# Expert sum of a hybrid decoder layer: 768 output columns of the second 128 tokens summed on VectorE from gathered expert rows

## The chip, the core and the metric

The kernel runs on one core of a Trainium2 chip. The metric is the device time of one execution in microseconds (us). Before the change, three runs took 2298.72, 2300.01 and 2301.34 us (median 2300.01).

## What is computed

One decoder layer for 256 tokens of width 2048, all in float32: a token mixer (sliding-window attention and an mLSTM, gated and merged), then a channel mixer of 16384 single-neuron experts. The change touches only the last part:

```python
# s_top, i_top: top 16 of 128 keys, for 8 heads and 2 halves; the 16 best of their 256 sums
idx   = ...                                # (256 tokens, 8 heads, 16): expert numbers
gates = softmax(top_s)                     # the same shape
u   = peer_u[idx]                          # expert rows, 2048 wide
act = gelu(einsum('td,thkd->thk', x, u))
out = einsum('thk,thkd->td', gates * act, peer_v[idx])
```

So each token has 128 slots (8 heads x 16); each slot is an expert with a weight, gate times gelu of a product, and the output is the weighted sum of the slots' rows of `peer_v`.

## The kernel before

The kernel does not gather expert rows. It multiplies all tokens with all 16384 rows of `peer_u`, multiplies gelu of that with a grid of gates that is zero where a token did not choose the expert, and multiplies the result with all of `peer_v`. Everything is a dense matrix product on TensorE.

A float32 matrix is split into two parts of TensorE's input type: `hi` (a rounded copy, made by ScalarE, L84) and `lo` (the remainder, made by VectorE, L85). A product is then three matmuls: hi by hi, hi by lo, lo by hi. All large matrices stream through the same buffers: `load` (L89) brings 128 rows of 1024 columns (512 KB) into one of four `raw` buffers by a DMA from SP's queue, `parts_of` splits them into two `hi` and two `lo` parts of 512 columns (four buffers each).

The stages follow each other: the mixer to about 690 us, the queries and scores to about 790, the u stage (128 expert blocks, each 128 rows of `peer_u`) to 1594, and the last stage with `peer_v` to the end.

- **u stage** (`ws_units`, L160 to L162): the weights stand, 256 tokens move. Per block 48 matmuls of 256 columns. The result, `z`, times the norm's factor goes to SBUF (L757), ScalarE takes its gelu (L748 or L750), and the product with the gates is kept for all blocks in `wA` and `wB` (128 experts of a block x 256 tokens). Beside it run the choice of the top 16 and `scatter` (L828 to L853), which spreads four tokens' gates over the grid: ScalarE and VectorE build one-hot factors in `ab` buffers, TensorE multiplies them.
- **Last stage** (`v_consume`, L865 to L880): per block the weights `wv(i)` are split into `ph` and `pl`, and stand on TensorE; the 2048 columns of `peer_v` move, 512 at a time. There are two halves of the tokens (t = 0, 1), so a block is 4 x 2 x 3 = 24 matmuls of 512 columns. The sums stay in all eight PSUM banks for the whole stage: `sd` for the first 128 tokens, `mm` for the second. At the end VectorE adds the residual `x1` (L891) and SP stores.

Work that may wait is kept in a list (`side`) and handed out between the units at a rate. Each engine then executes its instructions in one fixed order, which a scheduler computes from the program; an instruction whose wait is not yet fulfilled holds up all behind it on its engine.

## Time and profile before

| | |
|---|---|
| median of three runs | 2300.01 us |
| span of the profiled execution | 2296.5 us |
| TensorE busy | 2265.1 us, 99% |
| VectorE, ScalarE, GpSimd busy | 71%, 58%, 3% |
| DMA | 416.24 MB, 181 GB/s in the mean |
| last stage | 1594 to 2291 us |

The span is that of one execution taken by the profiler; the time of a run holds the start and the end of the program too. A busy TensorE counts a matmul from its start to its modelled end; since matmuls overlap, the time that one costs in a full queue is read from counts in a stretch, not from its duration. DMA-issuing instructions are not counted as busy time of the engine that issues them.

### The profile page before, as it was taken

Reading aid. Unit: us, or ns where it says so; the run is one execution under the profiler, and the core shown is the slowest. Engines: PE = TensorE matmul, PEld = TensorE weight load, DVE = VectorE, ACT = ScalarE, POOL = GpSimd, SP = SyncE. Lnnn points to the kernel's source line nnn. Section 1 sums busy time; section 2 is a strip of 40 time slices with the busy share of each in tenths; the row PEclk is TensorE's granted clock in tenths of the full one; section 3 lists DMA queues with packets and bytes.
Section 4 is the critical chain, followed back from the end, with each engine's and each line's share of the span. In section 5 each row is a group of like instructions: output and inputs, shape, how many; then the busy total and the mean of one; then the engine's idle time right before and its main releaser. Section 6 shows DMA issues by size and latency. Waiting matters only on the chain.

```text
span 2296.5 us, 41687 instructions
## 1 busy us (share of the span) xinstructions
PE 2265.1 (99%) x15441; PEld 2093.2 (91%) x15441; DVE 1640.0 (71%) x3436; ACT 1343.3 (58%) x2915; POOL 64.2 (3%) x79
## 2 busy tenths in 40 slices
PE   7999999999999999999999999999999999999998
PEld 6987799999999999999999999999888888888887
DVE  8977787677779996755677777786655555555555
ACT  6756566566554445554777777775555555555554
POOL 3000000000010020200000000000000000000000
PEclk9999999999999999999999999999999999999999
DMA  6565545556665545555554555556666666665665
GB/s 213 182 196 168 150 156 165 180 181 189 212 219 181 164 157 190 174 183 181 166 164 157 165 161 162 164 159 209 195 193 194 194 193 193 193 195 192 194 193 172
DMA packets 115339, 416.24 MB, mean 181 GB/s; under 512 B 12992, under 2 KB 13120, under 8 KB 114752
## 3 DMA queue, kind: packets, MB, share of 16 engines
q1 hardware_dynamic: 115136, 413.59, 56.5%
q8 instruction: 120, 1.97, 0.3%
q14 instruction: 83, 0.68, 0.1%
HBM read 409.35 MB, written 4.19 MB: 180 GB/s over the span
## 4 chain that ended last, share of the span: by engine, by line
PE 91%; DVE 6%; ACT 1%; issue 1%; POOL 0%; DMA 0%; DVEq 0%; SPq 0%; POOLq 0%; ACTq 0%
PE mm L162 17%; PE mm L160 17%; PE mm L161 17%; PE mm L880 5%; PE mm L878 5%; PE sd L878 5%; PE sd L880 5%; PE sd L879 5%; PE mm L879 5%; PE sd L841 2%; DVE lo L85 2%; PE mm L185 2%; PE mm L186 2%; PE mm L187 2%; ACT hi L84 1%
## 5 line engine op out<-in xcount | busy, mean ns | idle before, releaser
L85 DVE TENSOR_TENSOR lo<-raw,hi 128x512 fp32r<-128x512 f32 x1524 | 1056.2, 695 | 564.4 <-ACT hi L84 537.4
L84 ACT ACTIVATE hi<-raw 128x512 fp32r<-128x512 f32 x1524 | 954.4, 629 | 766.3 <-PE mm L161 374.4
L160 PE MATMUL mm<-xh,hi 128*128 128x256 f32 x3088 | 883.3, 286 | 9.9 <-ACT hi L84 7.4
L162 PE MATMUL mm<-xh,lo 128*128 128x256 f32 x3088 | 877.8, 284 | 9.3 <-DVE lo L85 8.9
L161 PE MATMUL mm<-xl,hi 128*128 128x256 f32 x3088 | 874.8, 283 | 1.1 <-DVE xl L85 1.1
L162 PEld LDWEIGHTS mm<-xh,lo 128*128 128x128 f32 x3088 | 592.2, 192 | 14.3 <-DVE lo L85 13.9
L160 PEld LDWEIGHTS mm<-xh,hi 128*128 128x128 f32 x3088 | 592.8, 192 | 11.5 <-ACT hi L84 8.1
L161 PEld LDWEIGHTS mm<-xl,hi 128*128 128x128 f32 x3088 | 592.9, 192 | 2.1 <-DVE xl L85 1.8
L879 PE MATMUL sd<-lo,ph 128*128 128x512 f32 x512 | 199.2, 389 | 0.0
L878 PE MATMUL sd<-hi,ph 128*128 128x512 f32 x512 | 199.2, 389 | 0.0
L878 PE MATMUL mm<-hi,ph 128*128 128x512 f32 x512 | 199.2, 389 | 0.0
L879 PE MATMUL mm<-lo,ph 128*128 128x512 f32 x512 | 199.2, 389 | 0.0
L880 PE MATMUL sd<-hi,pl 128*128 128x512 f32 x512 | 199.2, 389 | 0.0
L880 PE MATMUL mm<-hi,pl 128*128 128x512 f32 x512 | 199.2, 389 | 0.0
L880 PEld LDWEIGHTS mm<-hi,pl 128*128 128x128 f32 x512 | 96.1, 188 | 20.0
L878 PEld LDWEIGHTS mm<-hi,ph 128*128 128x128 f32 x512 | 96.1, 188 | 20.0
L879 PEld LDWEIGHTS sd<-lo,ph 128*128 128x128 f32 x512 | 96.1, 188 | 20.0
L880 PEld LDWEIGHTS sd<-hi,pl 128*128 128x128 f32 x512 | 96.1, 188 | 19.9
L879 PEld LDWEIGHTS mm<-lo,ph 128*128 128x128 f32 x512 | 96.1, 188 | 19.9
L878 PEld LDWEIGHTS sd<-hi,ph 128*128 128x128 f32 x512 | 96.1, 188 | 19.9
L835 ACT ACTIVATE ab<-iot,i1T 128x128 f32<-128x128 f32 x256 | 89.7, 387 | 0.5 <-DVE i1T L811 0.5
L185 PE MATMUL mm<-hi,xh 128*128 128x512 f32 x224 | 89.4, 400 | 0.0
(272 smaller groups left out, 2436.3 us busy)
## 6 DMA issues: line engine op xcount, KB each, us to landing
raw<-u SPq DMA_DIRECT2D x256, 512.0 KB, 3.8
raw<-v SPq DMA_DIRECT2D x256, 512.0 KB, 4.6
raw<-w_g SPq DMA_DIRECT2D x64, 512.0 KB, 4.0
raw<-w_tok SPq DMA_DIRECT2D x56, 512.0 KB, 4.2
raw<-w_qk SPq DMA_DIRECT2D x32, 512.0 KB, 3.9
raw<-w_o SPq DMA_DIRECT2D x32, 512.0 KB, 4.5
raw<-w_pq SPq DMA_DIRECT2D x32, 512.0 KB, 3.9
raw<-w_pa SPq DMA_DIRECT2D x16, 512.0 KB, 3.6
```

The costliest lines, as they stand in the source:

```text
L84: S.activation(hi, src, AF.Copy)
L85: V.tensor_sub(lo, src, hi.bitcast(F32))
L160: PE.matmul(ps, hi[:, w], xh[:, k], start=(k == 0), stop=False)
L161: PE.matmul(ps, hi[:, w], xl[:, k], start=False, stop=False)
L162: PE.matmul(ps, lo[:, w], xh[:, k], start=False, stop=(k == kts - 1))
L185: PE.matmul(ps, xh[:, k, ts], hi, start=(k == 0), stop=False)
L186: PE.matmul(ps, xh[:, k, ts], lo, start=False, stop=False)
L187: PE.matmul(ps, xl[:, k, ts], hi, start=False, stop=(k == KT - 1))
L835: S.activation(B, iot, AF.Square, bias=i1T[:, t:t + 1])
L878: PE.matmul(o, ph[:, ts], hi, start=(i == 0), stop=False)
L879: PE.matmul(o, ph[:, ts], lo, start=False, stop=False)
L880: PE.matmul(o, pl[:, ts], hi, start=False, stop=(i == NE - 1))
```

## The change

In the last stage the second 128 tokens keep 1280 of their 2048 columns on TensorE: in each block, for the third group of 512 columns only 256 move for them, for the fourth none. The other 768 columns come from gathered rows. In the u stage, each block's `z` of the second 128 tokens is stored to DRAM (`zd`) from ScalarE's queue, before gelu, which now writes to a buffer of its own (`gz`); the `zu` buffers go from two to four, the `ab` buffers from eight to six. When the choice of experts is done, `addresses` writes each slot's expert number and its address in `zd` to DRAM.

After the u stage these are read back into the space of `x2h` and `x2l` (named `xh` and `xl` in rows). GpSimd then issues indirect DMAs, 128 for the rows (slot s of 128 tokens: 128 rows of 768 columns from `vg`, a copy of the last 768 columns of `peer_v`) and 128 for `z` (one number per token each). Eight slabs hold rows. `gather(s)` multiplies slab s with the slot's weight and adds it to `accg` on VectorE; once per head of 16 slots ScalarE and VectorE make the weights. The next row into a slab is fetched when `gather` has read it. TensorE's block is 18 matmuls of 512 columns and 3 of 256.

```diff
@@ -30,6 +30,8 @@
 LOW = -3.0e38
 HU = 1024
 QU = 512
+DG = 1280
+GW = D - DG
 
 
 @with_exitstack
@@ -685,11 +687,16 @@
     finish_norm(sqa)
     mixer.close()
 
     X2 = (x2h, x2l)
     exc = pool(ctx, "exc", 1)
     NS = PH * TOPK
     iot = exc.tile([P, P], F32, name="iot")
+    tok = exc.tile([P, 1], F32, name="tok")
+    G.iota(tok, pattern=[[1, 1]], base=0, channel_multiplier=1, allow_small_or_imprecise_dtypes=True)
+    ixd = dram.tile([P, 2 * NS], U32, name="ixd")
+    gtd = dram.tile([P, NS], F32, name="gtd")
+    zd = dram.tile([NE * P * P, 1], F32, name="zd")
     G.iota(iot, pattern=[[1, P]], base=0, channel_multiplier=0, allow_small_or_imprecise_dtypes=True)
     gT = exc.tile([P, T], F32, name="gT")
     i0T = exc.tile([P, T], F32, name="i0T")
@@ -724,7 +731,7 @@
 
     def evac_q(n):
         def f(ps):
-            q = eb.tile([P, T], F32, name="zu")
+            q = eb.tile([P, T], F32, name="zu", bufs=4)
             V.tensor_mul(q, ps, rb)
             later.append(lambda: score(n, q))
         return f
@@ -747,13 +754,15 @@
         if k < T:
             S.activation(wv(i)[:, k:], z[:, k:], AF.Gelu)
         if k > 0:
-            S.activation(z[:, :k], z[:, :k], AF.Gelu)
-            V.tensor_mul(wv(i)[:, :k], wv(i)[:, :k], z[:, :k])
+            gz = eb.tile([P, T], F32, name="gz", tag="zu", bufs=4)
+            S.activation(gz[:, :k], z[:, :k], AF.Gelu)
+            V.tensor_mul(wv(i)[:, :k], wv(i)[:, :k], gz[:, :k])
+        S.dma_start(zd[i * P * P:(i + 1) * P * P, 0:1].rearrange("(p t) o -> p (t o)", t=P), z[:, P:T])
         done["e"] = i + 1
 
     def evac_u(i):
         def f(ps):
-            z = eb.tile([P, T], F32, name="zu")
+            z = eb.tile([P, T], F32, name="zu", bufs=4)
             V.tensor_mul(z, ps, rb)
             later.append(lambda: act_u(i, z))
         return f
@@ -811,11 +820,22 @@
         V.tensor_scalar(i1T[:, t * P:(t + 1) * P], pi[:, P:2 * P], -1.0, None, op0=OP.mult)
         V.tensor_copy(gT[:, t * P:(t + 1) * P], pi[:, 2 * P:3 * P])
 
+    def addresses():
+        ix = tk.tile([P, 2 * NS], U32, name="ix")
+        V.scalar_tensor_tensor(iv[:, 0], iv[:, 0], float(NK), iv[:, 1], op0=OP.mult, op1=OP.add)
+        V.tensor_copy(ix[:, 0:NS], iv[:, 0])
+        V.tensor_scalar(ix[:, NS:], iv[:, 0], float(P), tok, op0=OP.mult, op1=OP.add)
+        S.dma_start(ixd, ix)
+        S.dma_start(gtd, iv[:, 2])
     for t in range(NT):
         side += [lambda t=t, h=h: pick16(t, h) for h in range(PH)]
         side += [lambda t=t: decode(t), lambda t=t: gates(t)]
         side += [lambda t=t, c=c, h=h: lookup(t, c, h) for c in range(2) for h in range(PH)]
         side += [lambda t=t: turn(t)]
+        if t == NT - 1:
+            side.append(addresses)
     run(u_units(0, E0), 0.75)
     drain()
     tks.close()
@@ -823,10 +843,10 @@
     wpool = pool(ctx, "wpool", 1)
     W[1] = wpool.tile([P, NE - NA, T], F32, name="wB")
     TG = 4
-    NAB = 8
+    NAB = 6
 
     def scatter(t0):
         AB = []
         for j in range(TG):
             t = t0 + j
@@ -856,11 +876,56 @@
     run(u_units(E0, NE), 3 * len(side) / (2 * (NE - E0) - 5))
     drain()
 
-    acc = [[(psd, pmm)[t].tile([P, QU], F32, name=("sd", "mm")[t]) for q in range(4)] for t in range(NT)]
+    acc = [[psd.tile([P, QU], F32, name="sd") for q in range(4)],
+           [pmm.tile([P, QU], F32, name="mm") for q in range(3)]]
+    va = xx.tile([P, KT * T], F32, name="xh")
+    vb = xx.tile([P, KT * T], F32, name="xl")
+    AHEAD = 8
+    slab = [vb[:, j * GW:(j + 1) * GW] for j in range(5)] + [va[:, j * GW:(j + 1) * GW] for j in range(3)]
+    o0 = 3 * GW
+    accg = va[:, o0:o0 + GW]
+    wsl = va[:, o0 + GW:o0 + GW + NS]
+    zsl = va[:, o0 + GW + NS:o0 + GW + 2 * NS]
+    ixs = va[:, o0 + GW + 2 * NS:o0 + GW + 4 * NS].bitcast(U32)
+    nc.sync.dma_start(ixs, ixd)
+    nc.sync.dma_start(wsl, gtd)
+    def indirect(dst, table, ix):
+        G.indirect_dma_start(out=dst, out_offset=None, in_=table,
+                             in_offset=bass.IndirectOffsetOnAxis(ap=ix, axis=0))
+    def fetch_row(s):
+        indirect(slab[s % AHEAD], a["vg"], ixs[:, s:s + 1])
+    def fetch_z(h):
+        for s in range(h * TOPK, (h + 1) * TOPK):
+            indirect(zsl[:, s:s + 1], zd[:], ixs[:, NS + s:NS + s + 1])
+    def gather(s):
+        if s % TOPK == 0:
+            h = s // TOPK
+            hs = slice(s, s + TOPK)
+            S.activation(zsl[:, hs], zsl[:, hs], AF.Gelu)
+            V.tensor_mul(wsl[:, hs], wsl[:, hs], zsl[:, hs])
+            if h + 2 < PH:
+                fetch_z(h + 2)
+        w = wsl[:, s:s + 1]
+        if s == 0:
+            V.tensor_scalar(accg, slab[0], w, None, op0=OP.mult)
+        else:
+            V.scalar_tensor_tensor(accg, slab[s % AHEAD], w, accg, op0=OP.mult, op1=OP.add)
+        if s + AHEAD < NS:
+            fetch_row(s + AHEAD)
+    for s in range(AHEAD):
+        fetch_row(s)
+    fetch_z(0)
+    fetch_z(1)
+    side += [lambda s=s: gather(s) for s in range(NS)]
     pw = {}
-    x1 = xx.tile([P, NT, D], F32, name="xh")
-    nc.sync.dma_start(x1, x1d.rearrange("(t p) d -> p t d", p=P))
 
     def v_consume(i, h):
         def f(parts):
@@ -870,25 +935,37 @@
                 split(ph, pl, wv(i))
                 pw[i] = (ph, pl)
             ph, pl = pw[i]
-            for q in range(HU // QU):
-                hi, lo = parts[q]
+            for j in range(HU // QU):
+                q = h * 2 + j
+                hi, lo = parts[j]
                 for t in range(NT):
+                    n = QU if t == 0 else min(QU, DG - q * QU)
+                    if n <= 0:
+                        continue
                     ts = slice(t * P, (t + 1) * P)
-                    o = acc[t][h * 2 + q]
-                    PE.matmul(o, ph[:, ts], hi, start=(i == 0), stop=False)
-                    PE.matmul(o, ph[:, ts], lo, start=False, stop=False)
-                    PE.matmul(o, pl[:, ts], hi, start=False, stop=(i == NE - 1))
+                    o = acc[t][q][:, :n]
+                    PE.matmul(o, ph[:, ts], hi[:, :n], start=(i == 0), stop=False)
+                    PE.matmul(o, ph[:, ts], lo[:, :n], start=False, stop=False)
+                    PE.matmul(o, pl[:, ts], hi[:, :n], start=False, stop=(i == NE - 1))
         return f
 
     units = []
     for i in range(NE):
         for h in range(2):
             units.append((a["v"][i * P:(i + 1) * P, h * HU:(h + 1) * HU], v_consume(i, h)))
-    run(units)
-    for q in range(4):
+    run(units[:20], 0)
+    run(units[20:], NS / (len(units) - 30))
+    x1 = wA[:, 0:NT * D // T].rearrange("p i t -> p (i t)").rearrange("p (t d) -> p t d", d=D)
+    nc.sync.dma_start(x1, x1d.rearrange("(t p) d -> p t d", p=P))
+    drain()
+    V.tensor_add(x1[:, 1, DG:], accg, x1[:, 1, DG:])
+    for q in range(D // QU):
         for t in range(NT):
+            n = QU if t == 0 else min(QU, DG - q * QU)
+            if n > 0:
+                o = x1[:, t, q * QU:q * QU + n]
+                V.tensor_add(o, acc[t][q][:, :n], o)
             o = x1[:, t, q * QU:(q + 1) * QU]
-            V.tensor_add(o, acc[t][q], o)
             nc.sync.dma_start(out[t * P:(t + 1) * P, q * QU:(q + 1) * QU], o)
 
 
@@ -941,6 +1018,7 @@
         "keysT": z["peer_keys"].reshape(2 * PH, NK, P).transpose(2, 0, 1),
         "u": z["peer_u"].reshape(NE, P, KT, P).transpose(0, 3, 2, 1).reshape(NE, P, D),
         "v": z["peer_v"],
+        "vg": z["peer_v"][:, DG:],
     }
     arrays = {k: np.ascontiguousarray(v) for k, v in arrays.items()}
     nc = bacc.Bacc("TRN2", target_bir_lowering=False, num_devices=1)
```

VectorE in the last stage, before, a little over one block (`lo` the remainder of 512 columns of v, `pl` of the weights; what it waits for stands behind):

```order
L85 TENSOR_TENSOR lo<-raw,hi 128x512 [waits DMAHW1_49,Activation_49]
L85 TENSOR_TENSOR pl<-wA,ph 128x256 [waits PE_49,Activation_49]
L85 TENSOR_TENSOR lo<-raw,hi 128x512 [waits Activation_49]
L85 TENSOR_TENSOR lo<-raw,hi 128x512 [waits DMAHW2_49,Activation_49]
L85 TENSOR_TENSOR lo<-raw,hi 128x512 [waits Activation_49]
```

VectorE in the last stage, now, from the 52nd accumulation on (`xh` holds `accg` and three of the slabs, `xl` the other five):

```order
L918 SCALAR_TENSOR_TENSOR xh<-xl,xh 128x768 [waits DMASW7_49,DVE_49]
L87 TENSOR_TENSOR lo<-raw,hi 128x512 [waits DMAHW1_49,Activation_49]
L87 TENSOR_TENSOR lo<-raw,hi 128x512 [waits Activation_49]
L87 TENSOR_TENSOR pl<-wA,ph 128x256 [waits PE_49]
L87 TENSOR_TENSOR lo<-raw,hi 128x512 [waits DMAHW2_49,Activation_49]
L918 SCALAR_TENSOR_TENSOR xh<-xl,xh 128x768 [waits DMASW3_49,DVE_49]
L87 TENSOR_TENSOR lo<-raw,hi 128x512 [waits Activation_49]
L918 SCALAR_TENSOR_TENSOR xh<-xh 128x768 [waits DMASW5_49,DVE_49]
```

Accumulations (L918) that wait for a GpSimd DMA (DMASW) now stand between the `lo`, the first behind the 23rd of the stage's 512 `lo`, the 53rd (the second one shown) behind the 133rd, the 128th behind the 296th; behind that the order is as before.

GpSimd had nothing in the last stage; before, its queue ends with the lookups of the expert choice:

```order
L693 IOTA iot 128x128
L795 TENSOR_TENSOR oh<-oh,itf 128x256 x32
L950 UNCONDITIONAL_BRANCH
L950 ISA
```

GpSimd now, from its first DMA on (`vg` are row fetches, `zd` fetches of `z`; x48 is 48 in a row):

```order
L896 DMA xl<-vg,xh 128x768 x5
L896 DMA xh<-vg,xh 128x768 x3
L896 DMA xh<-zd,xh 128x1 x48
L896 DMA xl<-vg,xh 128x768 x5
L896 DMA xh<-vg,xh 128x768 x3
L896 DMA xl<-vg,xh 128x768 x3
L896 DMA xh<-zd,xh 128x1
L896 DMA xl<-vg,xh 128x768
L896 DMA xh<-zd,xh 128x1 x3
L896 DMA xl<-vg,xh 128x768
```

So 48 fetches of `z` stand ahead of the ninth row; the other 80 stand between the rows, all but the last ahead of the fetch for the 53rd accumulation, which is the 180th in the queue.

## Rows read from the trace of the kernel before

**Rows 1.** The page: busy time of the engines; granted TensorE clock in 40 slices.

```profile
PE 2265.1 (99%) x15441; PEld 2093.2 (91%) x15441; DVE 1640.0 (71%) x3436; ACT 1343.3 (58%) x2915; POOL 64.2 (3%) x79
...
PEclk9999999999999999999999999999999999999999
```

**Rows 2.** The page: the chain that ended last, by engine.

```profile
PE 91%; DVE 6%; ACT 1%; issue 1%; POOL 0%; DMA 0%; DVEq 0%; SPq 0%; POOLq 0%; ACTq 0%
```

**Rows 3.** Windows of u stage and last stage; columns in the first row.

```profile
core 0: us, PE busy (x) PEld busy (x) DVE busy (x) ACT busy (x) POOL busy (x), PEclk, DMA share, GB/s
1000.00:1100.00 100.00, 100.00 (x836) 100.00 (x836) 55.91 (x90) 50.21 (x87) 0.00 (x0) 1.00 0.57 183
1100.00:1600.00 500.00, 500.00 (x4185) 498.96 (x4184) 378.91 (x816) 363.86 (x1047) 0.00 (x0) 1.00 0.51 164
1594.00:2291.00 697.00, 696.56 (x3074) 576.44 (x3073) 410.79 (x644) 360.17 (x634) 0.00 (x0) 1.00 0.61 195
1900.00:2100.00 200.00, 200.00 (x885) 165.58 (x884) 117.39 (x184) 104.11 (x184) 0.00 (x0) 1.00 0.61 193
```

**Rows 4.** Waits in the last stage, 1620 to 2285 us: total, times, longest.

```profile
DVE lo L85 <- ACT hi L84: 236.9, 370, 0.7
ACT hi L84 <- DVE lo L85: 181.2, 249, 0.7
ACT hi L84 <- PE mm L880: 77.4, 120, 0.6
```

**Rows 5.** Line L89, last stage: duration of an issue in ns; landing in us.

```profile
L89 SPq DMA_DIRECT2D raw<-v x242: 327/328/328, 1620.1 to 2275.7; - x121
...
DMA to landing us min/median/max: 4.2/4.6/5.0
```

**Rows 6.** GpSimd by line and shape; line L795, ns min/median/max.

```profile
L795 POOL TENSOR_TENSOR oh<-oh,itf 128x256 f32<-128x256 f32 x32 | 30.9, 985 | 233.9 <-DVE oh L793 233.9
...
L795 POOL TENSOR_TENSOR oh<-oh,itf x32: 728/914/1579, 802.5 to 951.1; 128x256 f32<-128x256 f32 x32
```

**Rows 7.** VectorE by shape: last stage (two rows), whole span (two); busy, mean ns.

```profile
L85 DVE TENSOR_TENSOR lo<-raw,hi 128x512 fp32r<-128x512 f32 x486 | 336.9, 693 | 245.9 <-ACT hi L84 234.2
L85 DVE TENSOR_TENSOR pl<-wA,ph 128x256 fp32r<-128x256 f32 x72 | 30.6, 425 | 16.2 <-ACT ph L84 16.2
...
L85 DVE TENSOR_TENSOR ml<-gm,mh 128x256 fp32r<-128x256 f32 x16 | 6.7, 417 | 0.0
L499 DVE TENSOR_TENSOR s<-s,mx 128x1024 f32<-128x1024 f32 x4 | 4.9, 1225 | 0.1
```

**Rows 8.** Timeline of VectorE, back to back: start us, us.

```profile
15.87 0.68 DVE L85 TENSOR_TENSOR lo<-raw,hi 128x512 fp32r<-128x512 f32 x1
16.47 2.17 DVE L85 TENSOR_TENSOR xl<-xg,xh 128x256 fp32r<-128x256 f32 x3
```

**Rows 9.** Windows of 4 us with the fullest DMA; columns as in rows 3.

```profile
8.00:12.00 4.00, 1.38 (x4) 0.57 (x2) 4.00 (x8) 1.19 (x4) 3.12 (x4) 1.00 1.03 420
1600.00:1604.00 4.00, 4.00 (x19) 3.34 (x18) 2.44 (x4) 1.69 (x3) 0.00 (x0) 1.00 0.96 382
```

**Rows 10.** Waits in the u stage, 1100 to 1590 us: total, times, longest.

```profile
DVE ab L837 <- PE sd L841: 7.0, 19, 0.4
```

**Rows 11.** VectorE by shape, first 30 us (lo) and whole span (xl): mean ns.

```profile
L85 DVE TENSOR_TENSOR lo<-raw,hi 128x512 fp32r<-128x512 f32 x8 | 6.1, 772 | 0.2 <-ACT hi L84 0.2
...
L85 DVE TENSOR_TENSOR xl<-xg,xh 128x256 fp32r<-128x256 f32 x32 | 24.1, 771 | 0.5 <-ACT xh L84 0.5
```

## The prediction, made before the changed kernel was run

> **What bounds the kernel now.** I read the page's busy shares first, then the chain, then the stages by windows, then the waits and shapes of the last stage. The page gives TensorE 99% of the span with the granted clock at 2.4 GHz throughout [rows 1], and the chain that ended last is 91% TensorE [rows 2]: whatever leaves TensorE's queue shortens the run, as long as its operands still come in time. The stage that the change touches runs from 1594 to 2291 us: 696.6 us of TensorE for its 3072 matmuls of 512 columns, 0.2267 us each [rows 3]. An expert block (128 expert rows, two loads, four `lo` parts) is 24 of them, 5.44 us. In this stage VectorE works 410.8 of 697 us, ScalarE 360.2, GpSimd nothing [rows 3]. VectorE waits for ScalarE's `hi`, ScalarE for TensorE to give a buffer back [rows 4]; nobody is late.
>
> **TensorE: what goes.** Per block 24 matmuls of 512 columns become 18 of 512 and 3 of 256. In the u stage 836 matmuls, nearly all of 256 columns, fill 100 us, 0.1196 us each [rows 3]. So a block costs 18 x 0.2267 + 3 x 0.1196 = 4.44 us, and 128 blocks 568 us: 128.6 us less. This much is gained if VectorE, GpSimd and the DMA hide all that is added.
>
> **GpSimd: what comes, and how late.** 128 row fetches (128 rows of 3 KB each) and 128 `z` fetches (128 single numbers) go through GpSimd's queue, one behind the other. The order rows show what matters most: the scheduler put the 128 accumulations not over the whole stage but into 68 blocks. The 53rd stands behind 133 of the 512 `lo`, that is 33.25 blocks or 147.6 us into the stage; `lo` runs up to three parts ahead of TensorE, so it is due at about 144 us. Its row's fetch is the 180th in GpSimd's queue, behind 52 rows and 127 `z`. VectorE executes in order: if that row is late, the `lo` behind it, and TensorE with them, stand still.
> What does a fetch hold GpSimd for? No GpSimd DMA is in this trace. From below: SP's issue of a load, 0.33 us [rows 5]. From above: if each fetch held the queue to its landing, 4.6 us [rows 5]. Nearest in kind are GpSimd's own instructions over 128 partitions, programs like a fetch that builds 128 descriptors: the 32 multiplies `oh` take 0.728 us at least, 0.985 us in the mean, 1.579 us at most [rows 6]. I take 0.985. The start: index load after the last u matmul, about 3 us (an estimate from SP's 0.33 us and a landing under a large load's 4.6 us). The row lands 4.6 us after its issue. Due against come: 3 + 180 x 0.985 + 4.6 = 184.9 us, against 144: 41 us late. To this I add 10 us, an estimate: when accumulations run at the order's pace (4.44 us over 1.88 a block = 2.4 us), a row fetch waits for the slab read eight accumulations before, and the `z` behind it wait too, about four such gaps in the mixed part of the queue. GpSimd's part: 51 us. Behind the 53rd only one `z` is left; 75 more rows at one in 2.4 us are slower than 0.985 us, so the lateness does not grow.
> The Trainium skill, "DMA: Bandwidth & Descriptors", § Latency and other measured facts, has about 1 us to the first byte for a DMA issued from GpSimd, against 0.6 us from SP. No run here shows it; by that 1 us per fetch the late part would be 44 us in place of 41.
>
> **VectorE and the DMA in the gather blocks.** A block there has four `lo`, one `pl` and 1.88 accumulations of 768 columns. Durations: 0.693 and 0.425 us; 768 columns, between 0.693 (512) and 1.225 (1024), 0.96 us [rows 7]. Back to back they start closer than they last (`lo` at 15.87, the next at 16.47 us: 0.60 us for one that lasts 0.68 [rows 8]), so by pitch about 0.60, 0.34 and 0.87 us. A block is 4.38 us by pitch, 5.00 by duration, against TensorE's 4.44: over 68 blocks 0 to 38 us. The DMA: a block loads 1.05 MB of v and 1.88 x 0.393 MB of rows, 1.79 MB in 4.44 us, 403 GB/s. The trace reaches 382 and 420 GB/s for 4 us with its DMA engines full [rows 9], but in this stage's steady state 193 GB/s at a share of 0.61, 316 GB/s if full [rows 3]. While GpSimd is late there is less traffic, so this bites in the last 40 blocks: 1.79 MB at 382 GB/s is 4.69 us, 10 us in all; at 316 GB/s 49 us. Both causes stretch the same blocks, so I count them once: 15 us, nearer to the full-load rows.
>
> **What lies beside other work.** u stage: 128 stores of `z` issue from ScalarE at 0.33 us (SP's row), 42 us, on an engine that is idle 136 of 500 us there while TensorE is full [rows 3]: 0, and 42 us if that cover were gone. Six `ab` buffers for eight: the order keeps the `hi` ahead of the `ab` that wait, so 0; 64 scatters times 0.4 us, the longest wait seen for `sd` [rows 10], is the upper end, 26 us. The 2 MB load of `x1` still falls inside the stage, the accumulator's last add too; the final adds lose one of eight: 0.
>
> **Sum.** 568 + 51 + 15 = 634 us for the stage, 62.6 us less than 696.6. The profiled span is 2296.5 us; the runs' median 2300.0 lies 3.5 us above it, and that part stays. Forecast: 2237 us.
>
> **Rivals.**
> 1. *GpSimd is fast.* At 0.728 us a fetch, the shortest `oh`: 3 + 131 + 4.6 = 139 us, before the due 144. Nothing is late but the first gathers; 568 + 15 = 583 us, 2186 us; without the 15 us, 2171. For it: `z` fetches carry 512 bytes. Against: a fetch also reads 128 indices and builds 128 descriptors.
> 2. *GpSimd is slow: a wait in the place of the work removed.* The place is the same 180-deep queue. At 1.579 us, the slowest `oh`, the row comes at 292 us, 148 late; with the 10 us and VectorE then covered, 568 + 158 = 726 us, 2329 us. The kernel is slower than before from (128.6 + 144 - 7.6 - 10) / 180 = 1.42 us per fetch on. For it: `oh` ran beside a busy VectorE and spread from 0.73 to 1.58 us; the gather blocks keep VectorE fuller still.
> 3. *VectorE and GpSimd shut each other out.* In the first 30 us, beside GpSimd's multiplies and adds, `lo` takes 0.772 us, against 0.693 in the last stage, and `xl` 0.771 in the mean, against 0.417 for the same shape later [rows 7, 11]. If no accumulation or `lo` ran beside a fetch, the 68 blocks would need VectorE's 298 us plus GpSimd's 244 us (248 x 0.985), the other 60 blocks 266: 808 us, 2411 us. The Trainium skill, "SBUF — State Buffer", § SBUF: two separate sides, speaks against the change here: VectorE and GpSimd share a pair of ports as an exclusive lock, and a GpSimd that is locked out cannot write DMA descriptors; but it limits this for VectorE operations with two inputs to GpSimd work that reads SBUF. Rows 11 agree that GpSimd's elementwise work slows such operations; whether a fetch does, no row shows.
>
> **How the numbers follow.** Forecast's mechanism (lateness by a fetch between 0.75 and 1.42 us): 0.50. Rival 1: 0.25. Rival 2: 0.17. Rival 3: 0.05. The u stage's covers gone on top: 0.03. Differences under 0.2% count as no change. Faster: nearly all of the first two, 0.73; same: the edge near 1.42 us, 0.04; slower: 0.23. The range leaves out the very bottom of rival 1 and most of rival 3: 2180 to 2345 us.
>
> **What would show it.** In the changed kernel: matmuls of the last stage at 0.227 and 0.12 us, TensorE idle only in the first third of it, VectorE's idle before the accumulations ended by DMA or by GpSimd, GpSimd's queue full until about 190 us into the stage, then TensorE full or VectorE nearly so. DMA near 400 GB/s after that. Wrong, if TensorE's gaps lie in the u stage, if the accumulations last much over 0.96 us, if the loads of v land late, or if a fetch keeps GpSimd for under 0.75 or over 1.42 us.

## The result: 0.8% slower

The changed kernel takes 2318.35 us (median of four, 2313.50 to 2325.04) against 2300.49 us: ratio 1.0081, 95% interval 1.0062 to 1.0099. It is slower, where a faster kernel of 2237 us was forecast; the time lies inside the stated range, but on the other side of the kernel before. The profiled execution is the slowest of the four, 2325.04 us with a span of 2323.3.

The page of the changed kernel answers to [rows 1, 2]: busy time, granted clock, chain.

```profile
PE 2186.2 (94%) x15057; PEld 2000.2 (86%) x15057; DVE 1726.1 (74%) x3575; ACT 1325.7 (57%) x2923; POOL 371.3 (16%) x336
...
PEclk9999999999999999999999999999787799999999
...
PE 75%; DVE 8%; DMA 6%; POOL 5%; issue 4%; ACT 1%; DVEq 0%; SPq 0%; ACTq 0%; POOLq 0%
```

TensorE has 384 matmuls less and is 79 us less busy, but it no longer fills the span, and DMA, GpSimd and "issue" take 15% of the chain, where they had 1%. The windows, to be held against [rows 3]:

```profile
core 0: us, PE busy (x) PEld busy (x) DVE busy (x) ACT busy (x) POOL busy (x), PEclk, DMA share, GB/s
1100.00:1600.00 500.00, 500.00 (x4174) 497.69 (x4173) 378.99 (x815) 363.11 (x1048) 0.88 (x1) 1.00 0.54 172
1600.00:1850.00 250.00, 153.89 (x612) 117.55 (x610) 126.75 (x195) 75.88 (x148) 194.82 (x182) 0.81 0.62 214
1850.00:2050.00 200.00, 190.59 (x824) 143.78 (x825) 178.77 (x274) 105.25 (x200) 112.26 (x75) 0.98 0.95 345
2100.00:2300.00 200.00, 200.00 (x926) 164.11 (x925) 132.54 (x221) 119.92 (x221) 0.00 (x0) 1.00 0.70 231
```

The u stage is as before (4174 matmuls where there were 4185). The last stage has three parts, and counting matmuls tells what each loses. At full pace the changed block runs 926 matmuls in 200 us, 4.63 in a us (last row). From 1600 to 1850 us, 612 matmuls are 132 us of such work in 250 us: 118 us lost, with GpSimd's queue full (182 fetches, 194.8 us busy, since the profile does count these DMAs as busy time of GpSimd, and 0.30 us of gap before each). Of the 118 us TensorE is idle for 96; the other 22 go because the 612 matmuls took 153.9 us instead of 132, beside a granted clock of 0.81. From 1850 to 2050 us, 824 are 178 of 200: 22 us lost, with the DMA engines at a share of 0.95. After that nothing is lost.

Who waits, 1600 to 2310 us (total, times, longest):

```profile
DVE lo L87 <- ACT hi L86: 209.7, 203, 15.2
...
ACT xh L910 <- DMA xh<-zd,xh: 115.5, 8, 16.6
...
PE sd L947 <- ACT hi L86: 100.2, 18, 13.5
ACT hi L86 <- DMA raw<-v: 80.3, 55, 3.5
...
DVE xh L918 <- DMA xl<-vg,xh: 1.1, 2, 0.9
```

Against [rows 4], where no wait was longer than 0.7 us, there is a chain now: ScalarE's gelu of a head (L910) waits for its 16 `z`, up to 16.6 us; ScalarE's `hi` stand behind it, VectorE's `lo` behind those, TensorE behind both. The eight gelus waited 115.5 us in all. VectorE's accumulations (L918), whose wait the forecast was about, waited 1.1 us for rows. GpSimd's fetches (L896; ns min/median/max, first and last start), and on the timeline (start us, us, idle before) two of them from the first stretch and the 180th:

```profile
L896 POOL DMA_INDIRECT xh<-zd,xh x128: 943/947/1562, 1610.5 to 1848.0; - x128
...
L896 POOL DMA_INDIRECT xl<-vg,xh x80: 945/1154/2753, 1599.1 to 2042.6; - x80
```

```profile
1621.47 0.95 POOL L896 DMA_INDIRECT xh<-zd,xh  x1 [0.30 <-issue]
1622.72 0.95 POOL L896 DMA_INDIRECT xh<-zd,xh  x1 [0.30 <-issue]
...
1846.73 0.94 POOL L896 DMA_INDIRECT xl<-vg,xh  x1 [0.30 <-issue]
```

A fetch lasts 0.94 us at least, but the next begins 0.30 us after its end: 1.25 us from start to start. Longer ones bring the mean pitch of the first 180 to (1846.73 - 1599.1) / 179 = 1.38 us. The 180th is the one the forecast was about, the row of the 53rd accumulation. The next one, started at 1848.0 us, is the last `z`. On ScalarE and VectorE:

```profile
1851.31 0.22 ACT L910 ACTIVATE xh<-xh 128x16 f32<-128x16 f32 x1 [16.59 <-DMA xh<-zd,xh]
...
1852.08 2.04 DVE L87 TENSOR_TENSOR lo<-raw,hi 128x512 fp32r<-128x512 f32 x3 [15.23 <-ACT hi L86]
...
1865.96 1.01 DVE L918 SCALAR_TENSOR_TENSOR xh<-xl,xh 128x768 f32<-128x768 f32 x1
```

The first row is the gelu of the eighth head, which waits for that last `z`. It stands behind 121 of the stage's 512 `hi`, so TensorE needs the `hi` behind it after 30.25 blocks of 4.54 us, 137 us into the stage; it comes at 257. That is 120 us late, against 118 us that TensorE loses. The third row is the 53rd accumulation: it runs 272 us into the stage, where 144 was due, but it waited for nothing; its row had landed by 1857 us even with the longest landing of any fetch, 9.9 us.

### The profile page after: what moved, and what is told of

Read it like the earlier page. It is cut to its first block, busy times and chain, and to the rows that moved or that the text cites. A ratio compares the mean times of both kernels' runs of the same rounds, so it can differ in the third digit from the quotient of the medians.

```text
span 2323.3 us, 41940 instructions
## 1 busy us (share of the span) xinstructions
PE 2186.2 (94%) x15057; PEld 2000.2 (86%) x15057; DVE 1726.1 (74%) x3575; ACT 1325.7 (57%) x2923; POOL 371.3 (16%) x336
## 4 chain that ended last, share of the span: by engine, by line
PE 75%; DVE 8%; DMA 6%; POOL 5%; issue 4%; ACT 1%; DVEq 0%; SPq 0%; ACTq 0%; POOLq 0%
PE mm L164 17%; PE mm L162 17%; PE mm L163 17%; DMA raw<-v 4%; POOL xh L896 4%; DVE lo L87 4%; PE sd L948 3%; PE sd L947 3%; PE sd L949 3%; PE sd L861 3%; PE mm L187 2%; PE mm L188 2%; PE mm L189 2%; PE mm L947 2%; PE mm L949 2%
## 5 line engine op out<-in xcount | busy, mean ns | idle before, releaser
L947 PE MATMUL sd<-hi,ph 128*128 128x512 f32 x512 | 209.2, 409 | 100.2 <-ACT hi L86 100.2
L896 POOL DMA_INDIRECT xl<-vg,xh x80 | 104.6, 1308 | 721.4 <-PE sd L949 648.5
L948 PE MATMUL sd<-lo,ph 128*128 128x512 f32 x512 | 214.1, 418 | 6.0 <-DVE lo L87 5.5
L949 PE MATMUL sd<-hi,pl 128*128 128x512 f32 x512 | 206.3, 403 | 0.0
L896 POOL DMA_INDIRECT xh<-zd,xh x128 | 133.6, 1044 | 39.0 <-issue 35.4
L947 PE MATMUL mm<-hi,ph 128*128 128x512 f32 (+1 forms) x384 | 139.6, 363 | 0.0
L948 PE MATMUL mm<-lo,ph 128*128 128x512 f32 (+1 forms) x384 | 139.1, 362 | 0.0
L949 PE MATMUL mm<-hi,pl 128*128 128x512 f32 (+1 forms) x384 | 138.8, 362 | 0.0
L948 PEld LDWEIGHTS mm<-lo,ph 128*128 128x128 f32 x384 | 74.1, 193 | 18.2
```

The costliest lines, as they stand in the source:

```text
L896: G.indirect_dma_start(out=dst, out_offset=None, in_=table, in_offset=bass.IndirectOffsetOnAxis(ap=ix, axis=0))
L947: PE.matmul(o, ph[:, ts], hi[:, :n], start=(i == 0), stop=False)
L948: PE.matmul(o, ph[:, ts], lo[:, :n], start=False, stop=False)
L949: PE.matmul(o, pl[:, ts], hi[:, :n], start=False, stop=(i == NE - 1))
```

## Experiments

"Lost" is the time of a stretch less its matmuls at 4.63 in a us, where no other pace is given. Theory Q is that GpSimd's queue brings rows and `z` late against a fixed order on VectorE and ScalarE.

### TensorE's cut alone

```diff
-    for s in range(AHEAD):
-        fetch_row(s)
-    fetch_z(0)
-    fetch_z(1)
-    side += [lambda s=s: gather(s) for s in range(NS)]
+    V.memset(accg, 0.0)
```

> Leaves out all 256 fetches, the gelu, the multiplies and the accumulations (the gathered columns are 0); TensorE's share is cut as in the changed kernel, and the rows of the u products and their indices are still written. The forecast's first term alone: 128 blocks from 5.44 to 4.44 us, -128.6 us, 2165 to 2178 us. If the u stage had lost cover to the store of z, or if `v` can't be brought, split and used at a block of 4.44 us, it would be longer: above 2185 us.

Measured: 2187.30 us, ratio 0.9517 (0.9503 to 0.9531); the profiled execution 2185.9.

```profile
1900.00:2100.00 200.00, 200.00 (x925) 164.11 (x924) 132.49 (x220) 119.94 (x221) 0.00 (x0) 1.00 0.71 232
```

This is 9 us above its range and past the 2185 us that were to tell of a lost cover or a late `v`. Neither is seen: TensorE is full to the end, and the u stage has 4176 matmuls in the 500 us of [rows 3]. But the cut is worth 112 us, not 128.6: 925 matmuls in 200 us are 4.54 us per block, not 4.44. With this base the books close: 2185.9 + 118 + 22 = 2326 us, against 2325.04 in the profiled execution.

### Without `z`

```diff
-            S.activation(zsl[:, hs], zsl[:, hs], AF.Gelu)
-            V.tensor_mul(wsl[:, hs], wsl[:, hs], zsl[:, hs])
-            if h + 2 < PH:
-                fetch_z(h + 2)
...
-    fetch_z(0)
-    fetch_z(1)
```

> Leaves out the 128 fetches of z with their gelu and multiply: the slot weights are the gates alone; the 128 row fetches, the accumulations and TensorE's share stay. Theory Q (GpSimd's queue: 256 indirect fetches at a pitch of about 1.28 us, due faster than they can be issued): half of the queue goes and ScalarE's gelu no longer stands ahead of its `hi`, so the stretch 1600 to 1850 us loses its 120 us of TensorE's idle time but for 0 to 30; what is left is the DMA-bound stretch with its 25 us. Time 2190 to 2225 us. Theory X (VectorE's accumulations and GpSimd's work shut each other out of SBUF, or the accumulations are too long beside the `lo`): the accumulations are the same, so the loss stays; 2290 to 2320 us.

Measured: 2223.03 us, ratio 0.9665 (0.9648 to 0.9681).

```profile
1600.00:1950.00 350.00, 331.67 (x1441) 253.32 (x1441) 311.22 (x471) 182.73 (x344) 186.79 (x128) 0.98 0.96 355
```

With half the queue and the gelus gone 95 us come back, while VectorE does the same accumulations in less time: Q, not X. What is left, 39 us lost in these 350, lies under full DMA engines (0.96, 355 GB/s).

### Narrow rows

```diff
-        indirect(slab[s % AHEAD], a["vg"], ixs[:, s:s + 1])
+        indirect(slab[s % AHEAD][:, 0:64], a["vg"], ixs[:, s:s + 1])
```

> Each of the 128 row fetches brings 64 columns instead of 768 (the other columns of the slabs are set to 1 once, and the sum of those columns is not the expert sum); the number of fetches, the z fetches and the accumulations of 768 columns stay. Theory Q: GpSimd pays per fetch, not per byte, so the first stretch stays as it is (TensorE about 28 to 33 us busy of 50 from 1600 to 1800 us), rows land in about 3.5 instead of 7 us, and only the 25 us of the DMA-bound stretch come back: 2285 to 2300 us. Theory D (the gathered bytes, 50 MB on the DMA engines that also bring `v`, are what holds everything up): 2190 to 2215 us.

Measured: 2324.40 us, ratio 1.0107 (1.0090 to 1.0124).

```profile
1600.00:1850.00 250.00, 132.72 (x513) 102.26 (x512) 113.55 (x178) 66.68 (x131) 186.87 (x178) 0.75 0.38 119
1850.00:2050.00 200.00, 200.00 (x926) 164.08 (x925) 198.62 (x305) 120.00 (x221) 124.88 (x78) 1.00 0.78 244
```

Bytes are not the first stretch's trouble: it stalls with the DMA at 0.38. They are the second's, which now loses nothing. The total came 24 us above the range, since this edit let the scheduler place the first accumulations at `lo` 15 instead of 23, with 44 `z` in one piece behind the first eight rows: the first stretch loses 139 us instead of 118 and eats the gain. The second row also bears on rival 3. VectorE is busy 198.6 and GpSimd 124.9 of the same 200 us, so at least 123 us of both ran side by side; they do not shut each other out altogether.

### Every `z` twice

```diff
             indirect(zsl[:, s:s + 1], zd[:], ixs[:, NS + s:NS + s + 1])
+            indirect(zs2[:, s:s + 1], zd[:], ixs[:, NS + s:NS + s + 1])
```

> Every fetch of z is issued twice (the second copy goes to a tile that nobody reads): 384 instead of 256 indirect fetches, about 4 bytes per partition more each. Theory Q: GpSimd's queue sets the end of the first stretch, so 128 fetches at a pitch of 1.25 to 1.30 us are added to it, less what the DMA-bound stretch had cost: +130 to +165 us over the changed kernel, 2445 to 2485 us. Theory D (bytes): no change, 2315 to 2325 us. Theory X (VectorE's accumulations): 2315 to 2340 us.

Measured: 2431.47 us, ratio 1.0570 (1.0545 to 1.0594), 113 us over the changed kernel. Q in direction, against bytes and against VectorE. It is 14 us below the range: more rows moved into the stalled part (40 instead of 75 behind the last `z`), and with them, it seems, work of TensorE that overlapped the added fetches; no run tests this.

### Accumulations pinned to their program place

```diff
-    side += [lambda s=s: gather(s) for s in range(NS)]
+    def held(s):
+        with tc.issue_after(last["lo"].ins), tc.issue_after(last["hi"].ins):
+            gather(s)
+
+    side += [lambda s=s: held(s) for s in range(NS)]
```

`last` holds the instructions of the latest split.

> Same work, same instructions; VectorE's accumulation of a slot, and ScalarE's gelu, are pinned behind the `lo` and the `hi` that stand ahead of them in the program, where in the changed kernel the scheduler had moved them earlier. The 128 accumulations then lie over `lo` 23 to 480 instead of 23 to 296, so that 256 fetches are due in about 500 us of stage instead of 300. Theory Q: 256 x 1.28 = 328 us fit, and what stays is the start, where 48 z fetches stand ahead of the ninth row: 2200 to 2225 us. Theory X (accumulation and GpSimd shut each other out, or VectorE is too full): the same accumulations and the same overlap, 2290 to 2320 us. Theory D (bytes at the DMA engines): the bytes are spread more thinly, so it also gains, but only the 25 us of the DMA-bound stretch: about 2290 us.

Measured: 2278.76 us, ratio 0.9904 (0.9888 to 0.9921). A gain, but 54 us short of the range.

```profile
1600.00:1850.00 250.00, 181.40 (x731) 141.04 (x730) 131.12 (x208) 94.99 (x176) 178.70 (x168) 0.86 0.63 213
1850.00:2200.00 350.00, 349.54 (x1612) 285.63 (x1611) 301.48 (x476) 208.89 (x390) 130.89 (x86) 1.00 0.94 329
```

```profile
DVE xh L920 <- DMA xl<-vg,xh: 43.2, 5, 19.0
...
DVE xh L920 <- DMA xh<-vg,xh: 33.9, 6, 6.7
```

The first stretch still loses 92 us, now in VectorE's accumulations waiting for rows: this edit moves the gelus back too, and only the first of them still waits (10.9 us). The reason is the other order: on GpSimd the scheduler had put 48 `z` ahead of the ninth row and 66 ahead of the thirteenth. From 1850 us on there is room for all.

### GpSimd's order pinned too

```diff
-    for s in range(AHEAD):
-        fetch_row(s)
-    fetch_z(0)
-    fetch_z(1)
+    for s in range(TOPK):
+        fetch_z(s)
+    for s in range(AHEAD):
+        fetch_row(s)
...
+        if s + TOPK < NS:
+            fetch_z(s + TOPK)
```

The fetches are chained in this order.

> As the kernel with the accumulations pinned to their program place (2278.8 us), and GpSimd's 256 fetches pinned to program order too: 16 z, 8 rows, then one z and one row in turn, where 66 z fetches had stood ahead of the thirteenth row. Theory Q, second form (the loss is the lateness of each row against the place where VectorE must have it, so the order within GpSimd's queue counts as much as its length): only the start is late, 24 fetches x 1.28 us plus 7 us of landing = 38 us against an accumulation due at `lo` 15, 17 us into the stage, 21 us late; then the queue runs ahead. 2171 (before less the 128.6 us of TensorE) + 21 + 0 to 10 = 2190 to 2205 us. Rival R (any 256 fetches in this stage cost what they cost, whatever their order: the pace of GpSimd or its overlap with VectorE is the loss): as before the reordering, 2265 to 2285 us.

Measured: 2238.83 us, ratio 0.9735 (0.9722 to 0.9747): 40 us from the order of fetches (the first accumulations also moved, to `lo` 15 from `lo` 23), which rival R can't give, but 34 us above the range. 41 us are lost before 1750 us and 15 after.

The same, with the accumulations left to the scheduler:

> The order of GpSimd's fetches alone (16 z, 8 rows, then one z and one row in turn); VectorE's accumulations stay where the scheduler puts them, over `lo` 15 to 294, as in the changed kernel. Theory Q, second form: fetch n of the queue is issued at n x 1.28 us. Row 53 is then 114th (146 us, due 148), row 100 is 208th (266 + 7 us, due 245), the last 262nd (335 + 7, due 326): at most 28 us late from the queue; the DMA engines must move 71 MB of `v` and 50 MB of rows in that stretch, 341 us at 355 GB/s for 302 us of TensorE, 39 us late. The later of the two counts: 2171 + 39 + 0 to 15 = 2205 to 2225 us. Rival R (order of fetches is nothing, the dense accumulations are the loss): 2300 to 2325 us, as the changed kernel.

Measured: 2295.34 us, ratio 0.9980 (0.9969 to 0.9991). Q's number failed by 70 us, and this run alone would not refute rival R, whose range begins 5 us above. The 1.28 us per fetch that I put in were too few:

```profile
1650.00:2000.00 350.00, 295.74 (x1257) 235.49 (x1258) 270.94 (x413) 161.69 (x306) 263.51 (x210) 0.90 0.87 301
...
ACT xh L918 <- DMA xh<-zd,xh: 87.2, 8, 13.7
```

210 fetches in 350 us are 1.67 us each: 1.25 of work (`z` too, mixed with rows), 0.30 of gap, the rest waits for a slab, behind which the `z` stand as well. The 256 fetches (the expectation's 262 is a miscount) need 427 us at that pace, and the last is due after 326. Again it is the eight gelus that wait. So with the accumulations packed into 300 us, this order of the queue is worth 23 us; spread over 480 us, as in the run above, it is worth 40 us. Both orders count.

### First accumulation later

```diff
-    side += [lambda s=s: held(s) for s in range(NS)]
...
-    run(units[:20], 0)
-    run(units[20:], NS / (len(units) - 30))
+    run(units[:24], 0)
+    side += [lambda s=s: held(s) for s in range(NS)]
+    run(units[24:], NS / (len(units) - 34))
```

> As the kernel with both orders pinned, and the first accumulation moved from `lo` 15 to `lo` 44, 49 us into the stage, behind the 38 us that 24 fetches and a landing take. Theory Q, second form: nothing is late at the start either; 128 rows and the rest of `v` make 169 MB in 515 us, 328 GB/s against the 355 at which the DMA engines were full. 2171 + 0 to 10 = 2171 to 2185 us. Rival R: 2265 to 2285 us.

Measured: 2233.18 us, ratio 0.9683 (0.9651 to 0.9715), single runs from 2214 to 2237. 48 us above the range; 16 of them are its base, 2171 where the cut alone gives 2187. 27 us are lost before 1700 us, 23 after 1900. The latter have a name, ScalarE's gelu again, as this order issues the last `z` of a head one accumulation ahead of its gelu:

```profile
ACT xh L918 <- DMA xh<-zd,xh: 21.8, 6, 6.5
```

The former fall into the moment in which the eight first rows land:

```profile
1626.00:1634.00 8.00, 0.00 (x0) 0.00 (x0) 0.00 (x0) 0.40 (x1) 4.73 (x5) 0.50 0.95 359
1634.00:1638.00 4.00, 3.72 (x8) 2.70 (x9) 2.28 (x5) 2.48 (x6) 0.00 (x0) 0.50 0.03 9
```

VectorE, ScalarE and TensorE all stand still under full DMA engines, which shows that the two coincide, not that one causes the other (TensorE had thinned out before: 7 matmuls from 1620 to 1624 us, with the DMA at 0.32); the profile puts their waits down to "issue" and "remote", that is to nothing it shows.

### First rows spread, `z` 24 slots ahead

```diff
-    for s in range(TOPK):
-        fetch_z(s)
     for s in range(AHEAD):
+        fetch_z(2 * s)
+        fetch_z(2 * s + 1)
         fetch_row(s)
+    for s in range(TOPK, LEAD):
+        fetch_z(s)
...
-        if s + TOPK < NS:
-            fetch_z(s + TOPK)
+        if s + LEAD < NS:
+            fetch_z(s + LEAD)
```

> As the kernel with both orders pinned and the later start (2233 us, 46 us over TensorE's cut alone, 2187 us), with two edits of GpSimd's order: the first 8 rows go between pairs of z fetches, 3.8 us apart, where they had come 1.25 us apart and moved 3.15 MB in one go at 400 GB/s beside `v`, with VectorE, ScalarE and TensorE standing still for 10 us; and z is fetched 24 slots ahead, where the last z of a head had been issued one accumulation ahead of the gelu that reads it (`xh` waiting for z: 21.8 us in 6 waits). Theory Q, second form: both are lateness, and go: 2187 + 3 to 15 = 2190 to 2205 us. Rival R: the 46 us are what 256 fetches and 128 accumulations cost beside TensorE's work, wherever they stand: 2225 to 2238 us.

Measured: 2206.04 us, ratio 0.9596 (0.9572 to 0.9619), 1 us above the range (single runs from 2196 to 2218); rival R is out.

```profile
1600.00:1700.00 100.00, 86.86 (x369) 68.89 (x368) 60.84 (x100) 47.31 (x89) 58.61 (x53) 0.91 0.79 270
1700.00:2100.00 400.00, 400.00 (x1848) 328.48 (x1848) 348.36 (x548) 238.50 (x446) 245.44 (x197) 1.00 0.94 332
```

From 1700 us on nothing is lost, beside 197 fetches and VectorE at 87%. The start still loses 20 us. What stops it first, about 1640 us, I can't name; at 1669 us the 2 MB load of `x1` is issued, of which more below.

Now with 832 gathered columns:

> As the kernel with spread first rows and z 24 slots ahead, with 832 instead of 768 columns gathered (7 slabs instead of 8). TensorE's block loses 3 x 64 columns, about 10 us in all; the DMA engines have 169 MB to move in the 490 us in which rows are fetched, 346 GB/s, against 320 to 361 GB/s in the windows in which they were full. Theory Q, second form: 0 to 10 us shorter than with 768 columns if that holds; if the DMA engines are full, `v` comes late and it is 5 to 25 us longer.

Measured: 2227.92 us, ratio 0.9679 (0.9667 to 0.9692), 22 us longer: the second case by its time.

```profile
1600.00:1700.00 100.00, 73.86 (x311) 57.30 (x309) 49.26 (x80) 38.82 (x72) 51.20 (x46) 0.85 0.65 217
1700.00:2100.00 400.00, 397.01 (x1815) 322.24 (x1815) 346.98 (x537) 232.86 (x440) 264.02 (x195) 0.99 0.94 334
```

Full pace is 4.69 in a us here (164 matmuls from 2165 to 2200 us). The start loses 34 us instead of 20, and from 1700 to 2100 us 13 are lost with the DMA at 0.94, where 768 columns lost nothing. This points to DMA engines with little room beyond 768 columns, but doesn't show it: seven slabs instead of eight are part of the edit, and no run separates the two.

### TensorE's slower matmuls

In the cut kernels so far a 512-column matmul starts 0.2333 us after the one before it, not 0.2267.

> Leaves out the gather as the kernel with TensorE's cut alone, and 1024 columns of the second 128 tokens instead of 768, so that a block is 18 matmuls of 512 columns and none of 256. In the kernel before a 512-column matmul came every 0.2267 us, in the cut one every 0.233, with three of 256 columns at 0.117 between. Theory W (the three narrow matmuls slow those beside them): back to 0.2267, a block of 4.08 us, 2300 - 696.6 + 522 = 2126 us. Theory P (the pitch depends on something else that the cut changed, as two groups of the same kind following each other): 0.233, a block of 4.20 us, 2141 us.

Measured: 2143.38 us, ratio 0.9320 (0.9306 to 0.9333), and 0.2333: not the narrow matmuls.

> The kernel before with the same matmuls in another order: within a unit of 1024 columns the two column groups of the first 128 tokens follow each other, then the two of the second, where tokens had alternated. Nothing else is changed. Theory P (the 0.233 us of a 512-column matmul in the cut kernels comes from groups of the same 128 tokens following each other, which the cut brings about): 3072 matmuls x 0.0066 us = +15 to +20 us, 2315 to 2321 us, pitch 0.233. Theory N (the order is nothing; the cause lies elsewhere): 2298 to 2302 us, pitch 0.2267.

```diff
-            for q in range(HU // QU):
-                hi, lo = parts[q]
-                for t in range(NT):
+            for t in range(NT):
+                for q in range(HU // QU):
+                    hi, lo = parts[q]
```

Measured: 2300.51 us, ratio 1.0003 (0.9994 to 1.0013): not the order.

A version of the kernel before with one group less for the second 128 tokens, to tell unequal shares of the two halves of the tokens (theory M) from the rest of the change (theory B), gave no time. The next run tells them apart with equal shares:

> The changed kernel without the gather and without the cut: TensorE sums all 2048 columns for all tokens, 24 matmuls of 512 columns to a block as in the kernel before; the rows of the u products, their store and the index and gate loads stay, fetches, gelu, multiplies and accumulations are left out, and the output is that of the reference. Theory M: 0.2267 us, 2300 to 2303 us. Theory B: 0.2333 us, 2317 to 2323 us.

Measured: 2321.41 us, ratio 1.0089 (1.0072 to 1.0106). B: the slower pitch is in the changed program, whatever its width. One of its edits is a tile `tok` of 4 bytes per partition ahead of the last stage's buffers. I put it alone into the kernel before:

```diff
+    tok = exc.tile([P, 1], F32, name="tok")
+    G.iota(tok, pattern=[[1, 1]], base=0, channel_multiplier=1, allow_small_or_imprecise_dtypes=True)
```

> The kernel before with one tile more, `tok` of 4 bytes in each partition, where the changed kernel has it, and the one GpSimd instruction that fills it; nothing else is changed. Theory A: 3072 matmuls x 0.0066 us = +20 us, 2318 to 2323 us. Rival A0: 2298 to 2303 us.

Measured: 2319.79 us, ratio 1.0085 (1.0069 to 1.0100). Its window, against the 885 matmuls of [rows 3] in the same 200 us:

```profile
1900.00:2100.00 200.00, 200.00 (x858) 161.01 (x858) 113.87 (x179) 101.34 (x179) 0.00 (x0) 1.00 0.57 187
```

Four bytes cost 3% of TensorE's pace and 20 us. To pad the tile to 128 bytes does not undo it:

> The kernel without gather and without cut (2321 us, 0.2333 us per matmul), with one edit: the tile `tok`, 4 bytes in each partition, is allocated 128 bytes wide, so that the tiles behind it in SBUF (among them the buffers of `ph` and `pl`, TensorE's weights in the last stage) begin where they begin in the kernel before modulo 128 bytes. Theory A (TensorE's pitch depends on where its operands begin): 0.2267 us and 2299 to 2304 us. Rival A0 (not the place; fewer buffers of `ph` and `pl`, or another part of the change): 0.2333 us, 2319 to 2323 us.

Measured: 2318.32 us, ratio 1.0079 (1.0064 to 1.0095), 862 matmuls in 200 us. And in the best form:

> The kernel with spread first rows and z 24 slots ahead (2206 us) with the same edit, `tok` 128 bytes wide. Theory A: a block of 18 x 0.2267 + 3 x 0.114 = 4.42 us instead of 4.55, 128 blocks: 15 to 17 us less, 2184 to 2196 us. Rival A0: no change, 2200 to 2212 us.

Measured: 2194.03 us, ratio 0.9538 (0.9525 to 0.9551): 12 us less and in theory A's range, but not for its reason: the pitch is the slow one, and the start loses 8 us instead of 20. Why the padding does that stays open.

With `tok` moved among the short-lived tiles of the top-16 stage:

```diff
-    tok = exc.tile([P, 1], F32, name="tok")
...
+    tok = tk.tile([P, 1], F32, name="tok")
```

> The kernel with spread first rows and z 24 slots ahead, with `tok` (4 bytes in each partition) allocated among the short-lived tiles of the top-16 stage instead of ahead of the last stage's buffers, which so begin where they begin in the kernel before. Theory A: 512-column matmuls every 0.2267 us, a block of 4.42 instead of 4.55 us: 14 to 17 us less than the 2194 to 2206 us of the two forms with the shifted buffers, 2177 to 2192 us. Rival A0 (the place is not it): 2192 to 2208 us and 0.233 us.

Measured: 2187.18 us, ratio 0.9503 (0.9490 to 0.9516). This is the fastest version, 5% under the kernel before.

```profile
PE 2146.6 (98%) x15057; PEld 1995.8 (91%) x15057; DVE 1720.2 (79%) x3575; ACT 1327.9 (61%) x2923; POOL 382.4 (17%) x336
...
1700.00:2100.00 400.00, 399.04 (x1868) 331.10 (x1867) 349.10 (x553) 240.25 (x452) 239.74 (x192) 1.00 0.95 336
```

1868 matmuls in 400 us where there were 1848: 4.50 us per block against 4.55. At the pace of the last run below, 942 matmuls in 200 us or 4.71 in a us, the start (425 matmuls from 1600 to 1700 us) loses 10 us, and 9 of them in one place:

```profile
1660.00:1670.00 10.00, 6.87 (x33) 5.20 (x31) 3.26 (x6) 2.51 (x5) 7.56 (x9) 1.00 1.00 396
1670.00:1674.00 4.00, 0.00 (x0) 0.00 (x0) 0.00 (x0) 0.62 (x2) 0.88 (x1) 0.77 1.03 399
1674.00:1678.00 4.00, 3.94 (x9) 3.14 (x10) 3.38 (x5) 1.94 (x5) 1.17 (x2) 0.50 0.80 286
```

The 2 MB load of `x1`, needed only at the end, is issued at 1655.6 us and lands 15.1 us later, beside `v` and rows and under full DMA engines. That it is the cause is likely but not tested; to issue it after the last row would be the next thing to try.

With `tok` moved in the changed kernel:

> The changed kernel with that one edit, `tok` allocated elsewhere; fetches, orders and accumulations as they were. Theory A: the 0.13 us per block come back where TensorE sets the pace, about 79 of the 128 blocks (1850 us to the end), 10 us; in the first 250 us GpSimd's queue sets it and nothing comes back: 2303 to 2311 us. Rival A0: 2314 to 2325 us.

Measured: 2315.91 us, ratio 1.0065 (1.0050 to 1.0081): 2 us less, which is not clear of the noise, 5 above the range and inside that of A0. The pitch is back at the end of the stage (942 matmuls from 2100 to 2300 us, where there were 926), but GpSimd's queue sets the time of the rest. The place of a tile is not why the change failed.

## Why the prediction was wrong

The kernel was to be 63 us faster and is 18 us slower. Against the profiled execution, 88 us above the forecast, the terms missed by 67 (GpSimd), 16 (TensorE) and 7 us (VectorE and the DMA), which makes 90.

**TensorE, -128.6 us: mis-sized.** 112 us. The block came out at 4.54 us instead of 4.44. About 10 us of the difference are the place of `tok` (4.54 against 4.46 us, 128 blocks), which neither the order nor the trace of before could show; the small rest was not separated.

**GpSimd, 51 us: the step that failed, in its price and in the wait it was hung on.** 118 us. I took 0.985 us for a fetch, the mean of `oh` [rows 6], and let one start when the last ended; the trace has 1.38 us from start to start, 0.30 of it a gap that no busy time shows. 180 x (1.38 - 0.985) is 71 us, 54 of them the gap: by the forecast's own sum the row comes at 256 instead of 185 us, 112 us late instead of 41. That is the size of the loss, but the wait was another. The forecast had VectorE stand still for the row of its 53rd accumulation, and no term for the gelu, which stands in ScalarE's order ahead of `hi`. The trace has ScalarE standing still for `z`, 115.5 us in eight waits, and VectorE waiting for rows for 1.1 us. The two places lie close by luck: the last `z` is the 181st fetch, and its gelu stands behind 121 `hi`, three blocks ahead of the 133 `lo` of the forecast. The ten us for slabs did not come: until 1850 us no wait of GpSimd for VectorE was longer than the usual gap of 0.3 us.

The Trainium skill, "DMA: Bandwidth & Descriptors", § Latency and other measured facts, gives about 1 us to the first byte for a DMA from GpSimd. No row here shows a first byte; read as a price in GpSimd's queue, as the prediction tried it, 1 us is near the 0.94 us that a fetch lasts at least. The 0.30 us behind it and the 1.4 to 1.7 us of a mixed queue are not in it.

**VectorE and the DMA, 15 us: right, a little small.** 22 us, and narrow rows took them away, so it was the DMA: 345 GB/s at a share of 0.95, between the two bounds of 316 and 382, not the 400 of the signs. VectorE fits: an accumulation takes 1.01 us (0.96 estimated), and with narrow rows, at 99% busy, it still held TensorE's pace.

**The covers in the u stage: right.** Nothing was lost there. The load of `x1` in the last stage, put at nothing, may have cost 9 us in the fastest version; in the changed kernel (issued at 1702 us) it falls into the first stretch and can't be told from the rest.

**The rivals.** Rival 2 came, in its queue and nearly at its time (2329 us), with a chance of 0.17. The time is partly luck: it had put a fetch at 1.579 us and the lateness, with ten us for slabs, at 158; measured were 1.38 and 118, and TensorE's 16 us and the DMA's 22, which it took as covered, made up for it. The break-even was put at 1.42 us per fetch, so 1.38 alone would still have been faster; with 112 us for TensorE, 22 for the DMA and no slab waits it is (112 + 144 - 7.6 - 22) / 180 = 1.26 us, and 1.38 lies above.

Rival 3 is refuted as it stood, one after the other, by the 123 us of overlap. A weaker form stands. Counted over the changed kernel's trace, 81 fetches ran while VectorE did nothing, and they lasted 0.943 to 0.957 us; the other 175 lasted 1.32 us in the mean, up to 2.79. With narrow rows it is the same (95 fetches of 0.940 to 0.947 us, 161 of 1.38 in the mean), so bytes don't explain it. VectorE's own accumulations were not slowed, 1.003 to 1.055 us each. What in VectorE's work lengthens a fetch was not tested. The rule of the Trainium skill beside this rival ("SBUF — State Buffer", § SBUF: two separate sides), read as a bar on fetches beside accumulations, would have had them one after the other; the trace does not show that, as fetches of 0.94 us also ran beside a VectorE that was busy throughout.

The sum by what was measured: 2187 + 118 + 22 = 2327 us, against 2318 in the median and 2325 in the execution that was counted.

## What to carry to other kernels

When work moves to an engine whose instructions the trace has never shown, price its queue from start to start, and find the break-even price before choosing a value: here it lay inside the spread of the nearest row. Ask of each consumer, on every engine and not only the busiest, when its turn comes in the order and how many entries stand ahead of its producer: here the wait sat in eight short gelus on ScalarE, which no term held. Pinning both orders, fetching in the order of use and starting once the first fetches can have landed turned +0.8% into -4% with the same work, and the place of one tile made it -5%. And compare the pace of untouched instructions before and after: a 3% slower matmul pointed to four bytes.

## What the hardware showed unexpectedly

- An indirect fetch of 128 single numbers and one of 128 rows of 3 KB hold GpSimd alike, 0.943 and 0.945 us at least, with 0.30 us to the next; beside VectorE's work either was longer, 1.32 us in the mean of 175 fetches.
- With rows on top of `v`, the DMA engines moved 329 to 355 GB/s at shares of 0.94 to 0.96.
- TensorE's pitch for the same 512-column matmul is 0.2267 or 0.2333 us, depending on where the buffers behind a 4-byte tile begin; with 128 bytes of padding it was 0.232 (862 in 200 us). In the program `hi` and `lo` are allocated ahead of that tile, `ph` and `pl` behind it, which points to the weights; no run moved one operand alone.
- The granted clock fell where TensorE starved: 0.50 of full speed (1.2 of 2.4 GHz) from 1626 to 1634 us, with no matmul at all, and still 0.50 for the next 4 us, which held 8 matmuls instead of 18.
